# A hybrid decoder block on one core: the first stage scales x inside its transposing products, and moves part of its vector work

## The chip, the cores and the metric

The kernel runs on one core of a Trainium2 chip. The metric is the device time of one execution in microseconds (us). Engines: PE (TensorE, matrix products; PEld is its weight load), DVE (VectorE), ACT (ScalarE), POOL (GpSimd), SP (SyncE, which here only issues transfers). A name such as SPq or POOLq in a row is that engine's queue issuing a transfer.

## The reference

One decoder layer over 512 tokens of width 2048, all in float32. Only its first steps matter here:

```python
mod = jax.nn.silu(c) @ w_ada[l] + b_ada[l]              # c: (1, 2048), w_ada: 2048 x 12288
sh1, sc1, g1, sh2, sc2, g2 = jnp.split(mod, 6, axis=-1)
u = _modulate(_rmsnorm(h, norm_attn[l]), sh1, sc1)      # h * rsqrt(mean(h*h) + eps) * g, per token
z = u @ w_in                                            # 2048 x 5664
...
h = h + g1[:, None, :] * y                              # the plain h is needed again here
```

The rest (forgetting attention, sparse attention, the gated MLP, the last norm) is untouched by the change.

## The kernel before, in words

The program is one straight line per engine: every engine executes its own instructions in the order in which the Python code emits them, and waits at an instruction until its inputs are there. In the stage at hand the order is written out by hand, as a loop over steps.

**x.** x is 4 MB, as 4 blocks of 128 tokens (`t`), each loaded as two tiles of 128x1024 (L133) into the 8 buffers of the tag `adw`. PE transposes it in 128x128 pieces (L189, 64 transposes, 4 per PSUM bank); ACT and DVE copy the banks to `xT` (L194, L198), with channels on the partitions, and make the sums of squares beside it (L193, L196). When all four blocks are done, one short chain gives the token scale r = 1/sqrt(mean + eps) for all tokens (`rstd_of`, L163 to L169, a square root on ACT and one Newton step on DVE). PE broadcasts it over the partitions (`rows_of`, L175), and DVE multiplies it into each of the 16 channel tiles of xT (`norm_x`, L412), giving `xn`.

**w_ada.** The stage needs the first two of the six parts of mod (shift and scale): 32 MB of w_ada, in 64 slots of 512 KB. Slot n is loaded by SP (L513) into one of the 8 `adw` buffers as soon as its last user is done. 8 slots make a group `jj`, which gives 2x256 entries of mod, enough for two channel tiles. A slot holds two blocks of 128 rows. DVE multiplies each with its entry of silu(c) and adds it to `acc` (L538, L540). In 21 slots (`on_pe`) the second block goes to PE instead, as a 512-column product with a broadcast column (L550) whose row is copied (L554) and turned into columns (first half of L563). After a group, PE sums `acc` over the partitions as four single-column products (second half of L563), DVE adds the bias (`mod`, L571) and makes `a_vec` (L400), ACT makes u = xn * scale + shift twice (L418: a rounded high part and the full one), and DVE the low part (L423). The tables `LAGS` and `LAGS0` say how many steps after a group's last slot these follow.

**w_in.** Each tile of w_in is split into a high part (ACT, L244) and a low part (DVE, L249). A "unit" is three PE products of 128x512 (L278 to L280) into one bank. Units queue in `todo`; 1 to 3 are emitted per step, from step 39 on 3.

**Sine tables.** `tables` makes the cosine and sine tables for the rotary step in 19 pieces, 18 of them on DVE (L434 to L452); one piece is emitted per step, from step 14 on.

**The end of the stage.** SP writes the plain xT to DRAM (`xsp`, L602), since it is needed again much later, and the stage's memory is given up (`st.close()`). The rotary step of the keys (`roped`, L621 to L628) uses tiles in that memory, so it waits until those writes have landed; and PE's next products need the PSUM banks that it reads.

The code around the change, with the line numbers of the profile:

Of the kernel before, what the change touches and what calls it, by code (L numbers as in the profile page):

```python
# [29 lines left out]
LAGS0 = 1, 2, 3, 0  # L30
# [49 lines left out]
def hymba_block(ctx: ExitStack, tc: tile.TileContext, x, c, positions, w_ada, b_ada, norm_attn,  # L80
# [49 lines left out]
    for t in range(NT):  # L130
        for g in range(2):
            xt = early.tile([P, 2, T], F32, tag="adw", name=uid("xtok"), bufs=ADW)
            nc.sync.dma_start(xt, x[t * P:(t + 1) * P, g * 1024:(g + 1) * 1024].rearrange("p (a b) -> p a b", b=T))  # L133
            xtok[t, g] = xt
# [45 lines left out]
    ssq = con.tile([P, NT], F32, name="ssq")  # L180
    ssq4 = early.tile([P, NT, 4], F32, name="ssq4")
    xT = early.tile([P, ND, T], F32, name="xT")
    tags = BANKS_A + BANKS_B
    for t in range(NT):
        for g in range(4):
            src = xtok[t, g // 2][:, g % 2, :]
# [4 lines left out]
            junk = early.tile([P, T], F32, tag="mt", name=uid("junk"), bufs=2)  # L191
            if g % 2 == 0:
                nc.scalar.activation(junk, src, AF.Square, accum_out=ssq4[:, t, g:g + 1])  # L193
                nc.vector.tensor_copy(dst, b)  # L194
            else:
                nc.vector.scalar_tensor_tensor(junk, src, 1.0, src, op0=OP.mult, op1=OP.mult,  # L196
                                               accum_out=ssq4[:, t, g:g + 1])
                nc.scalar.copy(dst, b)  # L198
    nc.vector.tensor_reduce(ssq, ssq4, axis=AX.X, op=OP.add)
# [12 lines left out]
    rstd1 = rows_of(rstd_of(ssq, D, "rs1"), "mm", early.tile([P, T], F32, name="rstd1"))  # L212
# [196 lines left out]
    xn = [act.tile([P, T], F32, tag="al", name=f"xn{i}", bufs=ND) for i in range(ND)]  # L409

    def norm_x(i):
        nc.vector.tensor_tensor(xn[i], xT[:, i, :], rstd1, op=OP.mult)  # L412

    def modulate(i):
        h = act.tile([P, T], F32R, tag="ah", name=uid("uh"), bufs=ND)
        t = early.tile([P, T], F32, tag="mt", name=uid("mt"), bufs=2)
        for dst in (h, t):
            nc.scalar.activation(dst, xn[i], AF.Identity, scale=a_vec[:, 0, i:i + 1], bias=mod[:, i:i + 1])  # L418
        return h, t
# [8 lines left out]
    def tables():  # L428
        nonlocal cosT, sinT
        cosT = mid.tile([P, T], F32, tag="cos", name="cosT")  # L430
        sinT = mid.tile([P, T], F32, tag="sin", name="sinT")
        ang = posi.bitcast(F32)
        nc.scalar.copy(ang, posi)
        nc.vector.tensor_scalar(ang, ang, cs[:, K_FRQ:K_FRQ + 1], None, op0=OP.mult)  # L434
        yield
        for dst, turn in ((sinT, 0.0), (cosT, 0.25)):
            kk = mid.tile([P, T], F32, tag="wx", name=uid("kk"))
# [59 lines left out]
    def on_pe(n):  # L497
        j, r = divmod(n, 8)
        return r < 5 if j == 0 else j <= HJ and 2 <= r < 6

    tiles, accs, rows, sums, halves, fetched, todo = {}, {}, {}, {}, {}, {}, []
    extra_work = tables()
    AT, AT_END = {0: 0, 1: 1, 3: 2}, {0: 0, 1: 1, 5: 2}
    norms = {4: (0, 1), 5: (2,), 6: (3,), 8: (4, 5)}
    norms.update({9 + i: (6 + i,) for i in range(10)})
    step = 0
    while step < SLOTS + 8 or todo:
        j, r = divmod(step, 8)
        if j < NJ:
            tiles[step] = early.tile([P, 2, T], F32, tag="adw", name=uid("ad"), bufs=ADW)  # L510
            for i, sec in ((0, 1), (1, 0)):
                c0 = sec * D + j * 256
                nc.sync.dma_start(tiles[step][:, :, i * 256:(i + 1) * 256],  # L513
                                  w_ada[:, c0:c0 + 256].rearrange("(q p) n -> p q n", p=P)[:, 2 * r:2 * r + 2, :])
# [15 lines left out]
        if 0 <= n < SLOTS:  # L530
            jj, q0 = n // 8, 2 * (n % 8)
            if q0 == 0:
                accs[jj] = early.tile([P, T], F32, tag="acc", name=uid("acc"), bufs=2)
            acc = accs[jj]
            for q in range(1 if on_pe(n) else 2):
                sc1 = sl[:, q0 + q:q0 + q + 1]
                if q0 + q == 0:
                    nc.vector.tensor_scalar(acc, tiles[n][:, q, :], sc1, None, op0=OP.mult)  # L538
                else:
                    nc.vector.scalar_tensor_tensor(acc, tiles[n][:, q, :], sc1, acc, op0=OP.mult, op1=OP.add)  # L540
        if step in norms:
            for i in norms[step]:
                norm_x(i)
        n = step - 2
        if 0 <= n < SLOTS and on_pe(n):
            jj, q = n // 8, 2 * (n % 8) + 1
            first = n == 0 or not on_pe(n - 1)
            if first:
                rows[jj] = bank("mm")
            nc.tensor.matmul(rows[jj], sl[:, q:q + 1].to_broadcast([P, P]), tiles[n][:, 1, :],  # L550
                             start=first, stop=not on_pe(n + 1))
            if not on_pe(n + 1):
                row = early.tile([1, T], F32, tag="row", name=uid("row"), bufs=2)
                nc.scalar.copy(row, rows[jj][0:1, :])  # L554
                rows[jj] = row
        n = due(step, 0)
        if n is not None:
            jj = n // 8
            sums[jj] = bank("mm")
            srcs = ([(rows.pop(jj), one_col[0:1, :])] if jj in rows else []) + [(accs.pop(jj), one_col)]  # L560
            for av, one in srcs:
                for i in range(4):
                    nc.tensor.matmul(sums[jj][:, i:i + 1], av[:, i * P:(i + 1) * P], one,  # L563
                                     start=i == 0 and one is srcs[0][1], stop=one is one_col,
                                     skip_group_check=True)
# [28 lines left out]
        if step >= 14:  # L594
            next(extra_work, None)
# [5 lines left out]
    for i in range(ND):  # L601
        nc.sync.dma_start(xsp[i], xT[:, i, :])  # L602
# [836 lines left out]
```

## Time and profile before

| | |
|---|---|
| median of 3 runs | 2440.64 us (2437.82 to 2442.27) |
| the profiled execution | 2438.08 us, its span 2436.3 us, mean granted clock of PE 0.977 |
| busy over the span | PE 2349.1, DVE 1583.2, ACT 1026.5, POOL 341.2 us |
| the stage at hand | from 0 to about 180 us of the span |

All times of the trace count from the start of the span. PE is busy nearly everywhere, but a busy PE need not be a fast one, since the ends of products are modelled and its clock has two levels: a granted clock of 1.0 is 2.4 GHz, 0.5 is 1.2 GHz. So the stage is read engine by engine, by what each waits for.

### The profile page before, as it was taken

The page shows a single profiled execution, that of the slowest core. Times are in us where ns is not written, and L with a number is a line of the kernel's source. Part 1 is how long each engine was busy: PE and PEld are TensorE (multiplying, and loading weights), DVE is VectorE, ACT ScalarE, POOL GpSimd, SP SyncE. Part 2 cuts the span into 40 slices and gives each one's busy share as a digit, 9 for nine tenths or more (in the row PEclk, how much of TensorE's full clock was granted, in tenths as well). Part 3 has the DMA queues.
Part 4 walks back from the last instruction along what each step waited for, and adds up shares of the span by engine and source line. Part 5 has one row for each costly group of instructions (what it writes and reads, how often), then busy time and mean ns, then how long its engine had stood idle before and what let it go on. Part 6 is the DMA issues. An engine that isn't in the chain of part 4 may idle for free.

```text
span 2436.3 us, 38417 instructions
## 1 busy us (share of the span) xinstructions
PE 2349.1 (96%) x14677; PEld 2100.5 (86%) x14677; DVE 1583.2 (65%) x2719; ACT 1026.5 (42%) x1544; POOL 341.2 (14%) x370
## 2 busy tenths in 40 slices
PE   6998999999999999889999999999999999999998
PEld 4777887888887777789999999999999888888887
DVE  7867887787655566596777677777676633333333
ACT  3335444334323323365555555555555422222233
POOL 0002002000102021251222221212121100000010
PEclk8999999999999999899999999999999999999998
DMA  9974643453563287469898889988988644333322
GB/s 331 322 232 143 178 142 101 122 180 119 164 181 122 82 274 255 159 145 231 214 230 220 221 217 229 224 219 219 216 200 196 187 156 141 121 117 122 105 94 99
DMA packets 322713, 440.31 MB, mean 181 GB/s; under 512 B 26224, under 2 KB 217552, under 8 KB 322528
## 3 DMA queue, kind: packets, MB, share of 16 engines
q1 hardware_dynamic: 289104, 348.21, 44.3%
q0 software_dynamic: 31120, 85.45, 18.9%
q10 hardware_dynamic: 2304, 4.20, 0.5%
q8 instruction: 115, 1.88, 0.3%
q14 instruction: 70, 0.57, 0.1%
HBM read 340.18 MB, written 28.38 MB: 151 GB/s over the span
## 4 chain that ended last, share of the span: by engine, by line
PE 55%; DVE 1%; DMA 0%; issue 0%; ACT 0%; SPq 0%; DVEq 0%; ACTq 0%
PE py L1173 12%; PE py L1176 11%; PE py L1175 11%; PE psmm L278 3%; PE psmm L280 3%; PE psmm L279 3%; PE pss L278 2%; PE pss L279 2%; PE pss L280 2%; PE pso L278 1%; PE pso L279 1%; PE pso L280 1%; DMA wr<-in_w_down_dram 0%; PE pso L1070 0%; DVE ul L1153 0%
## 5 line engine op out<-in xcount | busy, mean ns | idle before, releaser
L249 DVE TENSOR_TENSOR wl<-wr,wh 128x1024 fp32r<-128x1024 f32 (+2 forms) x211 | 238.8, 1132 | 371.1 <-ACT wh L244 369.5
L244 ACT CAST wh<-wr 128x1024 fp32r<-128x1024 f32 (+2 forms) x211 | 199.7, 948 | 528.9 <-PE psmm L279 204.0
L1176 PE MATMUL py<-uh,ls 128*128 128x256 f32 x1408 | 398.4, 283 | 2.8 <-DVE ls L1119 2.8
L1173 PE MATMUL py<-uh,hs 128*128 128x256 f32 x1408 | 399.3, 284 | 0.9 <-DVE ev L1190 0.5
L1175 PE MATMUL py<-ul,hs 128*128 128x256 f32 x1408 | 398.4, 283 | 1.8 <-DVE ul L1153 1.8
L1113 ACT CAST hs<-sum 128x1024 fp32r<-128x1024 f32 x176 | 184.6, 1049 | 377.0 <-PE py L1175 256.6
L1119 DVE TENSOR_TENSOR ls<-sum,hs 128x1024 fp32r<-128x1024 f32 x176 | 215.3, 1223 | 196.3 <-ACT hs L1113 196.3
L1175 PE MATMUL py<-ul,hx 128*128 128x256 f32 x1056 | 298.7, 283 | 4.1 <-DVE ul L1153 4.1
L1173 PE MATMUL py<-uh,hx 128*128 128x256 f32 x1056 | 299.3, 283 | 1.7 <-ACT uh L1152 1.4
L1176 PE MATMUL py<-uh,lx 128*128 128x256 f32 x1056 | 298.3, 282 | 0.0
L1176 PEld LDWEIGHTS py<-uh,ls 128*128 128x128 f32 x1408 | 268.0, 190 | 3.6 <-DVE ls L1119 3.6
L1173 PEld LDWEIGHTS py<-uh,hs 128*128 128x128 f32 x1408 | 268.1, 190 | 2.7 <-DVE ev L1190 1.3
L1175 PEld LDWEIGHTS py<-ul,hs 128*128 128x128 f32 x1408 | 268.0, 190 | 2.7 <-DVE ul L1153 2.7
L1109 POOL DMA_DIRECT2D lx<-raw x176 | 156.1, 887 | 579.2 <-ACT lx L1108 431.8
L1175 PEld LDWEIGHTS py<-ul,hx 128*128 128x128 f32 x1056 | 200.8, 190 | 4.9 <-DVE ul L1153 4.8
L1173 PEld LDWEIGHTS py<-uh,hx 128*128 128x128 f32 x1056 | 200.6, 190 | 2.2 <-ACT uh L1152 1.7
L1176 PEld LDWEIGHTS py<-uh,lx 128*128 128x128 f32 x1056 | 200.6, 190 | 0.0
L386 DVE SCALAR_TENSOR_TENSOR acc<-ad,sl,acc 128x512 f32<-128x512 f32 x180 | 143.2, 796 | 41.7 <-DMA ad<-in_w_ada_dram 40.1
L1108 ACT ACTIVATE lx<-raw 128x768 fp32r<-128x768 f32 x176 | 148.0, 841 | 1.8 <-DMA raw<-in_w_gate_dram 1.8
L1104 ACT CAST hx<-raw 128x768 fp32r<-128x768 f32 x176 | 144.4, 820 | 9.0 <-DMA raw<-in_w_gate_dram 9.0
L278 PE MATMUL psmm<-fh,wh 128*128 128x512 f32 x352 | 137.0, 389 | 0.0
L280 PE MATMUL psmm<-fh,wl 128*128 128x512 f32 x352 | 136.9, 389 | 0.0
(442 smaller groups left out, 5290.4 us busy)
## 6 DMA issues: line engine op xcount, KB each, us to landing
lx<-raw POOLq DMA_DIRECT2D x176, 384.0 KB, 5.2
ad<-in_w_ada_dram SPq DMA_DIRECT2D x128, 512.0 KB, 3.9
raw<-in_w_up_dram SPq DMA_DIRECT2D x176, 256.0 KB, 4.1
raw<-in_w_gate_dram SPq DMA_DIRECT2D x176, 256.0 KB, 4.4
wr<-in_w_down_dram SPq DMA_DIRECT2D x88, 512.0 KB, 3.7
ad<-in_w_ada_dram SPq DMA_DIRECT2D x128, 256.0 KB, 6.0
wr<-in_w_in_dram SPq DMA_DIRECT2D x104, 256.0 KB, 3.4
wr<-in_w_in_dram SPq DMA_DIRECT2D x24, 512.0 KB, 4.9
```

What stands on the lines that cost most here:

```text
L244: nc.scalar.copy(wh[:, :, sc], v)
L249: nc.vector.tensor_tensor(held[1][:, :, sc], v, split_ap(held[0])[:, :, sc], op=OP.subtract)
L278: nc.tensor.matmul(dst, wh[:, k, w], ah, start=first, stop=False)
L279: nc.tensor.matmul(dst, wh[:, k, w], al, start=False, stop=False)
L280: nc.tensor.matmul(dst, wl[:, k, w], ah, start=False, stop=last)
L1108: nc.scalar.activation(lx[s], raw[s][:, 1:4, :], AF.Copy, scale=-1.0)
L1109: nc.gpsimd.dma_start(split_ap(lx[s]), raw[s][:, 1:4, :], accum_op=OP.add)
L1113: nc.scalar.copy(hs[s], sums[s])
L1119: nc.vector.tensor_tensor(ls[s], sums[s], split_ap(hs[s]), op=OP.subtract)
L1173: nc.tensor.matmul(o, wh[:, wi, js], vh[:, vi, :], start=k == 0 and j == 0, stop=False, skip_group_check=True)
L1175: nc.tensor.matmul(o, wh[:, wi, js], vl[:, vi, :], start=False, stop=False, skip_group_check=True)
L1176: nc.tensor.matmul(o, wl[:, wi, js], vh[:, vi, :], start=False, stop=k == KG - 1, skip_group_check=True)
```

## The change

- x is loaded as 16 tiles of 128x512 into buffers of the tag `al` (free until the first low parts of u), so the 8 `adw` buffers are free for w_ada from the start.
- Each block of 128 tokens gets its own token scale (`token_scale`: nine DVE operations and a square root on ACT), which is put on the diagonal of a 128x128 tile. `turn` multiplies each piece of x with that diagonal as an ordinary fp32 product: this transposes and scales at once. Three of four banks are copied by ACT and one by DVE (before: half each). `norm_x`, `xn` and the broadcast at the start are gone. `std` keeps 1/r.
- PE's share of w_ada falls from 21 to 14 blocks (slots 0 to 5, 10 to 13, 18 to 21), and is made like the sum of `acc`: four products of one column each, straight into the group's bank. The 512-column products, their rows and the copies are gone.
- `LAGS0` is 1, 1, 2 in place of 1, 2, 3.
- The tables start at step 60 in place of 14, two pieces per step.
- At step 56 PE broadcasts `std`; from step 66 on DVE multiplies two tiles of xT per step with it, which gives the plain x again, and POOL (not SP) writes each to `xsp`.

```diff
-LAGS0 = 1, 2, 3, 0
+LAGS0 = 1, 1, 2, 0
+TAB = 60
...
+    def token_scale(t):
+        v, r, s = (early.tile([P, 1], F32, name=uid("rs1")) for _ in range(3))
+        nc.vector.tensor_reduce(v, ssq4[:, t, :], axis=AX.X, op=OP.add)
+        nc.vector.tensor_scalar(v, v, 1.0 / D, EPS, op0=OP.mult, op1=OP.add)
+        nc.scalar.activation(s, v, AF.Sqrt)
...
+        nc.vector.scalar_tensor_tensor(r, s, 1.5, r, op0=OP.add, op1=OP.mult)
+        diag = early.tile([P, P], F32, tag="diag", name=uid("diag"), bufs=2)
+        nc.vector.tensor_scalar(diag, ident, r, None, op0=OP.mult)
+        nc.vector.scalar_tensor_tensor(std[:, t:t + 1], v, -2.0, r, op0=OP.mult, op1=OP.mult)
+        return diag
+
+    def turn(t, diag):
+        for g in range(4):
             b = bank(tags[(t * 4 + g) % 8], (P, 4, P))
             for i in range(4):
-                nc.tensor.transpose(b[:, i, :], src[:, i * P:(i + 1) * P], ident)
+                nc.tensor.matmul(b[:, i, :], xtok[t, g][:, i * P:(i + 1) * P], diag, start=True, stop=True)
...
+    squares(0)
+    for t in range(NT - 1):
+        diag = token_scale(t)
+        squares(t + 1)
+        turn(t, diag)
...
-        return r < 5 if j == 0 else j <= HJ and 2 <= r < 6
+        return r < 6 if j == 0 else j < 3 and 2 <= r < 6
...
+    def plain_x(i):
+        nc.vector.tensor_tensor(xT[:, i, :], xT[:, i, :], stdr[0], op=OP.mult)
+        nc.gpsimd.dma_start(xsp[i], xT[:, i, :])
+
+    for n in range(3):
+        load_ada(n)
+    diag = token_scale(NT - 1)
+    accumulate(0)
+    turn(NT - 1, diag)
...
-            nc.tensor.matmul(rows[jj], sl[:, q:q + 1].to_broadcast([P, P]), tiles[n][:, 1, :],
-                             start=first, stop=not on_pe(n + 1))
...
+            columns(n // 8, tiles[n][:, 1, :], sl[:, q:q + 1], False)
...
-        if step >= 14:
-            next(extra_work, None)
+        if step >= TAB:
+            for _ in range(2):
+                next(extra_work, None)
+        if step == SLOTS - 8:
+            std_row()
+        if step >= SLOTS + 2:
+            for _ in range(2):
+                if plain:
+                    plain_x(plain.pop(0))
...
-    for i in range(ND):
-        nc.sync.dma_start(xsp[i], xT[:, i, :])
```

Where the order of an engine's instructions matters, it stands here as the programs have it; numbers behind a name count tiles.

DVE, between the last token scale and the first group's sums. Before:

```order
L168 TENSOR_TENSOR rs1s<-rs1s,rs_259 128x4
L169 SCALAR_TENSOR_TENSOR rs1r<-rs1s,rs1r 128x4
L538 TENSOR_SCALAR acc_308<-ad_302,sl 128x512
L540 SCALAR_TENSOR_TENSOR acc_308<-ad_305,sl,acc_308 128x512
L540 SCALAR_TENSOR_TENSOR acc_308<-ad_310,sl,acc_308 128x512
L540 SCALAR_TENSOR_TENSOR acc_308<-ad_316,sl,acc_308 128x512
L412 TENSOR_TENSOR xn_278<-xT,rstd_269 128x512
L412 TENSOR_TENSOR xn_279<-xT,rstd_269 128x512
```

and now:

```order
L203 SCALAR_TENSOR_TENSOR rs_71_312<-rs_72_313,rs_71_312 128x1
L205 TENSOR_SCALAR diag_322<-cs,rs_71_312 128x128
L206 SCALAR_TENSOR_TENSOR std<-rs_70_311,rs_71_312 128x1
L540 TENSOR_SCALAR acc_325<-ad_302,sl 128x512
L216 COPY xT<-pso_345 128x4x128
L542 SCALAR_TENSOR_TENSOR acc_325<-ad_305,sl,acc_325 128x512
L542 SCALAR_TENSOR_TENSOR acc_325<-ad_308,sl,acc_325 128x512
L542 SCALAR_TENSOR_TENSOR acc_325<-ad_357,sl,acc_325 128x512
```

One slot's product now stands between the diagonal and a copy from PSUM of the last products made with it, and the rest of the group stands behind that copy. In the three blocks ahead, the two squares of the next block (L191) stand in its place.

DVE again, at the end of the stage, from the last slot's sum on. Before:

```order
L249 TENSOR_TENSOR wl_1324<-wr_1241,wh_1323 128x768
L571 TENSOR_TENSOR mod<-psmm_1342,vec 128x2 x2
L400 SCALAR_TENSOR_TENSOR a_vec<-mod,vec 128x2
L423 TENSOR_TENSOR ul_1385<-mt_1360,uh_1359 128x512
L423 TENSOR_TENSOR ul_1387<-mt_1364,uh_1363 128x512
L249 TENSOR_TENSOR wl_1339<-wr_1246,wh_1338 128x1024
```

and now:

```order
L273 TENSOR_TENSOR wl_1347<-wr_1252,wh_1346 128x768
L459 TENSOR_SCALAR kk_1362<-kk_1362 128x512
L461 TENSOR_SCALAR kk_1362<-kk_1362 128x512
L601 TENSOR_TENSOR mod<-psmm_1368,vec 128x2 x2
L424 SCALAR_TENSOR_TENSOR a_vec<-mod,vec 128x2
L465 SCALAR_TENSOR_TENSOR cosT<-kk_1362,posi 128x512
L465 SCALAR_TENSOR_TENSOR cosT<-kk_1362,cosT 128x512
L558 TENSOR_TENSOR xT<-xT,stdr 128x512 x2
L465 SCALAR_TENSOR_TENSOR cosT<-kk_1362,cosT 128x512 x2
L558 TENSOR_TENSOR xT<-xT,stdr 128x512 x2
L442 TENSOR_TENSOR ul_1425<-mt_1388,uh_1387 128x512
```

Pieces of the tables (L457 to L471) stand on both sides of the last `mod`, and the 16 products that restore x (L558) stand behind it, two by two between the rest of the tables, the low parts and the next splits of w_in.

PE, at the first group of w_ada. Before:

```order
L175 MATMUL psmm_270<-cs,rs1r 128x128 x4
L550 MATMUL psmm_314<-ad_302,sl 128x512
L550 MATMUL psmm_314<-ad_305,sl 128x512
L550 MATMUL psmm_314<-ad_310,sl 128x512
L550 MATMUL psmm_314<-ad_316,sl 128x512
L550 MATMUL psmm_314<-ad_321,sl 128x512
L563 MATMUL psmm_363<-cs,row_341 128x1 x4
L563 MATMUL psmm_363<-cs,acc_308 128x1 x4
```

and now:

```order
L213 MATMUL pso_345<-diag_322,xtok_113 128x128 x4
L549 MATMUL psmm_352<-sl,ad_302 128x1 x4
L549 MATMUL psmm_352<-sl,ad_305 128x1 x4
L549 MATMUL psmm_352<-sl,ad_308 128x1 x4
L549 MATMUL psmm_352<-sl,ad_357 128x1 x4
L549 MATMUL psmm_352<-sl,ad_365 128x1 x4
L549 MATMUL psmm_352<-sl,ad_373 128x1 x4
L549 MATMUL psmm_352<-cs,acc_325 128x1 x4
```

The single-column products of six slots stand behind the last block's products with the diagonal; before, five 512-column products stood behind one short broadcast.

## Rows read from the trace of the kernel before

**Rows 1.** Busy time of each engine in three stretches; columns as headed.

```profile
core 0: us, PE busy (x) PEld busy (x) DVE busy (x) ACT busy (x) POOL busy (x), PEclk, DMA share, GB/s
23.79:154.15 130.36, 120.42 (x491) 90.58 (x492) 122.94 (x198) 44.87 (x59) 0.00 (x0) 0.91 0.98 316
38.30:65.00 26.70, 21.37 (x78) 14.56 (x79) 26.52 (x46) 8.83 (x12) 0.00 (x0) 0.88 1.08 347
65.00:157.60 92.60, 92.60 (x396) 72.40 (x395) 83.06 (x129) 33.32 (x43) 0.00 (x0) 0.94 0.92 295
```

**Rows 2.** Timeline, last slot and last group: start, duration, engine, line, [idle before <- releaser].

```profile
152.62 1.53 DVE L540 SCALAR_TENSOR_TENSOR acc<-ad,sl,acc 128x512 f32<-128x512 f32 x2
...
157.67 0.95 PE L563 MATMUL psmm<-cs,acc 128*128 128x1 f32 x8
...
158.65 0.23 DVE L571 TENSOR_TENSOR mod<-psmm,vec 128x2 f32<-128x2 f32 x2 [3.63 <-PE psmm L563]
```

**Rows 3.** Line L602 by itself, and the timeline where the stage is left.

```profile
L602 SPq DMA_DIRECT2D xsp<-xT x16: 423/649/934, 164.3 to 174.8; - x16
...
179.00 0.59 ACT L621 ACTIVATE sw<-psmm 64x512 f32<-64x512 f32 x1 [2.84 <-DMA xsp<-xT]
...
180.97 0.63 PE L278 MATMUL psmm<-uh,wh 128*128 128x512 f32 x1 [2.30 <-DVE r L623]
```

**Rows 4.** Timeline of the start, from the first tile of x to the first unit.

```profile
6.79 0.63 ACT L193 ACTIVATE junk<-xtok 128x512 f32<-128x512 f32 x1 [2.93 <-DMA xtok<-in_x_dram]
...
9.30 0.63 ACT L193 ACTIVATE junk<-xtok 128x512 f32<-128x512 f32 x1
...
18.28 1.47 PE L189 MATMUL pss<-cs,xtok 128*128 128x128 f32 x12
...
21.50 1.28 ACT L164 ACT_TABLE_LOAD   x1
...
21.88 0.17 DVE L199 TENSOR_REDUCE ssq<-ssq 128x4 f32<-128x16 f32 x1
...
23.03 0.17 DVE L165 TENSOR_SCALAR rs<-rs 128x4 f32<-128x4 f32 x1 [0.57 <-ACT rs1s L164]
...
23.79 0.49 DVE L538 TENSOR_SCALAR acc<-ad,sl 128x512 f32<-128x512 f32 x1
...
23.92 1.87 PE L175 MATMUL psmm<-cs,rs1r 128*128 128x128 f32 x8 [3.21 <-DVE rs1r L169]
...
38.34 0.80 PE L278 MATMUL pss<-uh,wh 128*128 128x512 f32 x1 [2.37 <-ACT uh L418]
```

**Rows 5.** Busy time of each engine around L175; columns as in rows 1.

```profile
23.80:27.20 3.40, 3.28 (x10) 2.33 (x11) 3.29 (x7) 0.58 (x1) 0.00 (x0) 0.56 1.10 348
```

**Rows 6.** Timeline of PE: a 512-column product of w_ada, and single columns.

```profile
34.23 1.73 PE L563 MATMUL psmm<-cs,acc 128*128 128x1 f32 x8 [1.48 <-DVE acc L540]
...
98.25 0.40 PE L280 MATMUL pss<-uh,wl 128*128 128x512 f32 x1
98.49 1.02 PE L550 MATMUL psmm<-ad,sl 128*128 128x512 f32 x2
...
99.58 0.39 PE L279 MATMUL pss<-ul,wh 128*128 128x512 f32 x1
...
103.55 1.05 PE L563 MATMUL psmm<-cs,row 1*128 1x1 f32 x8
104.53 1.05 PE L563 MATMUL psmm<-cs,acc 128*128 128x1 f32 x8
```

**Rows 7.** Groups by line, DVE, 23.8 to 151.6: count | busy us, mean ns | idle.

```profile
L540 DVE SCALAR_TENSOR_TENSOR acc<-ad,sl,acc 128x512 f32<-128x512 f32 x97 | 72.7, 750 | 2.2
...
L412 DVE TENSOR_TENSOR xn<-xT,rstd 128x512 f32<-128x512 f32 x16 | 10.8, 684 | 0.0
...
L446 DVE SCALAR_TENSOR_TENSOR sinT<-kk,sinT 128x512 f32<-128x512 f32 x3 | 2.1, 687 | 0.0
```

**Rows 8.** Line L1109, POOL's transfers beside a busy DVE: ns minimum/median/maximum, and landing.

```profile
L1109 POOL DMA_DIRECT2D lx<-raw x176: 847/849/1175, 960.5 to 1908.2; - x176
...
DMA to landing us min/median/max: 3.9/5.2/8.1
```

More of the change, by code (lines that the diff above doesn't have):

```diff
@@ L130, in hymba_block @@
     for t in range(NT):
[L131 to L134, printed above, removed]
+        for g in range(4):
+            xtok[t, g] = act.tile([P, T], F32, tag="al", name=uid("xtok"), bufs=ND)
+            nc.sync.dma_start(xtok[t, g], x[t * P:(t + 1) * P, g * T:(g + 1) * T])
     rows1 = early.tile([P, P], F32, name="rows1")
@@ L498, in on_pe, with load_ada, accumulate, columns @@
         j, r = divmod(n, 8)
-        return r < 5 if j == 0 else j <= HJ and 2 <= r < 6
-    tiles, accs, rows, sums, halves, fetched, todo = {}, {}, {}, {}, {}, {}, []
+        return r < 6 if j == 0 else j < 3 and 2 <= r < 6
+    tiles, accs, sums, halves, fetched, todo = {}, {}, {}, {}, {}, []
     extra_work = tables()
     AT, AT_END = {0: 0, 1: 1, 3: 2}, {0: 0, 1: 1, 5: 2}
-    norms = {4: (0, 1), 5: (2,), 6: (3,), 8: (4, 5)}
-    norms.update({9 + i: (6 + i,) for i in range(10)})
+    def load_ada(n):
+        j, r = divmod(n, 8)
+        tiles[n] = early.tile([P, 2, T], F32, tag="adw", name=uid("ad"), bufs=ADW)
+        for i, sec in ((0, 1), (1, 0)):
+            c0 = sec * D + j * 256
+            nc.sync.dma_start(tiles[n][:, :, i * 256:(i + 1) * 256],
+                              w_ada[:, c0:c0 + 256].rearrange("(q p) n -> p q n", p=P)[:, 2 * r:2 * r + 2, :])
+    def accumulate(n):
+        jj, q0 = n // 8, 2 * (n % 8)
+        if q0 == 0:
+            accs[jj] = early.tile([P, T], F32, tag="acc", name=uid("acc"), bufs=2)
+        acc = accs[jj]
+        for q in range(1 if on_pe(n) else 2):
+            sc1 = sl[:, q0 + q:q0 + q + 1]
+            if q0 + q == 0:
+                nc.vector.tensor_scalar(acc, tiles[n][:, q, :], sc1, None, op0=OP.mult)
+            else:
+                nc.vector.scalar_tensor_tensor(acc, tiles[n][:, q, :], sc1, acc, op0=OP.mult, op1=OP.add)
+    def columns(jj, src, one, last):
+        first = jj not in sums
+        if first:
+            sums[jj] = bank("mm")
+        for i in range(4):
+            nc.tensor.matmul(sums[jj][:, i:i + 1], src[:, i * P:(i + 1) * P], one,
+                             start=first and i == 0, stop=last, skip_group_check=True)
+    stdr = []
+    def std_row():
+        stdr.append(rows_of(std, "mm", early.tile([P, T], F32, name="stdr")))
+    def plain_x(i):
[6 more added lines that the diff above has]
+    turn(NT - 1, diag)
+    plain = list(range(ND))
     step = 0
@@ L508, in hymba_block @@
         j, r = divmod(step, 8)
[L509 to L514, printed above, removed]
+        if j < NJ and step not in tiles:
+            load_ada(step)
         if r == (3 if j else 7) and j < NJ:
@@ L529, in hymba_block @@
         n = step - 1
[L530 to L543, printed above, removed]
+        if 1 <= n < SLOTS:
+            accumulate(n)
         n = step - 2
         if 0 <= n < SLOTS and on_pe(n):
[L546 to L549, printed above, removed]
-            nc.tensor.matmul(rows[jj], sl[:, q:q + 1].to_broadcast([P, P]), tiles[n][:, 1, :],
-                             start=first, stop=not on_pe(n + 1))
[L552 to L555, printed above, removed]
+            q = 2 * (n % 8) + 1
+            columns(n // 8, tiles[n][:, 1, :], sl[:, q:q + 1], False)
         n = due(step, 0)
         if n is not None:
[L558 to L565, printed above, removed]
+            columns(n // 8, accs.pop(n // 8), one_col, True)
         n = due(step, 1)
@@ L600, in hymba_block @@
             z_first[0] = lambda w=w: w
-    for i in range(ND):
-        nc.sync.dma_start(xsp[i], xT[:, i, :])
+    for i in plain:
+        plain_x(i)
+    for _ in extra_work:
+        pass
     st.close()
```

31 lines of the change are left out of this document (16 added, 15 removed).

## The prediction

> **What bounds the kernel now.** I read four views: the busy times by stretch, the timeline of the stage's two ends, the groups of DVE's instructions, and the timeline of the start.
>
> Backwards from the end: PE stops at 178.7 and goes on only at 180.97, when DVE has read a bank of the rotary step; that step on ACT had waited until 179.0 for the last write of `xsp` [rows 3]. The writes stand behind the last group's `mod`, at 158.65. So the stage is left 179.0 - 158.65 = 20.35 us after the last `mod`, whatever was fast before. Call the last `mod` M.
>
> What sets M? DVE is busy 122.94 of the 130.36 us from its first slot of w_ada (23.79) to the end of its last one, 152.62 + 1.53 = 154.15 [rows 1, 2]. The transfers run beside it at a share of 0.98, 316 GB/s, and PE is busy without a gap from 65 on [rows 1]. The last sum over the partitions starts on PE at 157.67, and DVE waits 3.63 us for it [rows 2]. So three chains end close together: DVE's work, PE some 3 us behind it, and the transfers a little ahead. A gain on one is capped by the next. The reader should see here that DVE was the chain to relieve, and that relief only counts if DVE starts as early as before.
>
> **The change, part by part.**
>
> *DVE's work between its first and last slot of w_ada.* The 16 `norm_x` go: 10.8 us of busy time [rows 7], some 10.3 without the overlap of neighbours. Ten of the 18 table operations move behind the last slot: four of the eight large ones at 0.687 [rows 7] and six small ones; with overlap I put it at 4.5 (bounds 4 and 5). Seven slots' second blocks come back from PE: 7 x 0.75 = 5.2 [rows 7]. The first slot's product (0.5) is done earlier. 122.9 - 10.3 - 4.5 + 5.2 - 0.5 = 112.8 us of work: 10.1 less.
>
> *When this work can start.* Before: at 23.79, right behind the token scale. Now the rest of the first group stands behind the copy of the last block's products, and so do, block after block, the next scale, products and copy. DVE cannot step over a copy that waits for PE, so the four blocks add up:
> - The first block is there at about 8.5 (its first half before 6.79, its second by 9.30, [rows 4]). A square 0.8, the table load 1.3 and the root 0.2 on ACT give 10.8. From the root to the finished scale DVE took 0.9 (23.03 to 23.92), the diagonal adds 0.3 (an estimate from the small operations): the products start at 12.0.
> - One product: four 128x128 fp32 products took 1.87 us at a granted clock of 0.56, so near 1.2 GHz: 0.43 each with the tail off [rows 4, 5]. At 2.4 GHz no row shows one. The nearest is the 512-column one: from 98.25 to 99.58 are two ordinary products of 0.23 and it, so 0.87, a quarter of which is 0.22 [rows 6]. Sixteen take 6.9 us at the low clock, 3.5 at the high one. PE has idled before the first block, so I take 5.2 there (the clock rises halfway), and 4.2 for the others, between 3.5 and 6.9 and nearer the first, since PE pauses only some 2.6 us between blocks.
> - So copy of block 0 done at 12.0 + 5.2 + 0.7 = 17.9. Each further block: scale 1.9 (reduce, small operations and root as in [rows 4], no table load, diagonal), products 4.2, copy 0.7: 6.8. Two small copies add 0.5. 17.9 + 3 x 6.8 + 0.5 = 38.8, say 39.
>
> The start moves from 23.8 to 39: 15.2 us later. Bounds: 34.5 (first products at 11, 3.5 throughout after a first 4.5), and 48.6 (6.9 everywhere).
>
> The Trainium skill says, in "TensorE: Matmul & The Clock Gate", Terms, that the transpose mode is "4× faster for FP32"; this change leaves that mode. By that rule a product would cost four of the transposes' 1.47 / 12 = 0.12 us [rows 4], 0.49, and a block 7.8, which by itself would put the start near 51. The row of L550 (0.22) speaks against it.
>
> *What DVE waits for after that.* Nine sums end near 46. PE then has single columns to finish: eight records took 1.73 us after a pause and 0.9 to 0.98 in the midst of work [rows 6]; six slots from 38.3 on take between 5.5 and 10.4, I take 8, and the sum over `acc` 1.7: first `mod` at 48, two us after DVE is free (36.9 before), first unit at 49.5 in place of 38.34 [rows 4]. With 1.5 us for other waits (before: 7.4 in all, most of them for PE) the last slot ends at 39 + 112.8 + 3.5 = 155.3, before 154.15.
>
> *PE.* Behind its first unit it loses 16 products of 0.87 and four rows of 0.98, 17.8, and gets eight slots of 0.92 and the broadcast of `std` (0.9): 9.5 less. It starts 11.2 later, but had idled 26.70 - 21.37 = 5.3 in the first stretch [rows 1]. 157.67 - 9.5 + 11.2 - 5.3 = 154.1: now just ahead of DVE, so its saving is not on the path.
>
> *Transfers.* x no longer occupies the w_ada buffers, so slots 0 to 7 and the first w_in tiles are loaded by about 29 (9.3 MB at 350 GB/s). Then slot 8 waits for slot 0's users, near 39: this head start is thrown away. 38 MB are left; at the 347 GB/s of [rows 1] they end near 148, 7 us ahead of DVE's end. SP has only these loads behind it. Cost 0; the cover is DVE's 155.
>
> *M.* Behind the last slot DVE has a split and four small table operations, 2.4 us: M = 157.7, against 158.65: 0.95 earlier.
>
> *From M to leaving the stage.* DVE: `mod` 0.4, six table operations 3.1, two low parts 1.3, two splits 2.3, sixteen plain tiles 10.3 (as `norm_x`): 17.4. POOL issues each write while DVE makes the next; behind them on POOL stand only the rotary products, which wait for the writes anyway. Landing 4.1 to 5.2 after an issue (179.0 less 174.8 on SP's queue, [rows 3]; 5.2 on POOL's, [rows 8]): 21.5 to 22.6, in place of 20.35. I take 1.6 us longer. ACT's copies (12 instead of 8) and the later sine step lie beside it: 0.
>
> **Sum.** -0.95 + 1.6 = +0.7 us. The profiled execution took 2438.08, 2.6 under the median of 2440.64, so 2438.8 to 2441.3: I forecast **2440 us**, no change that can be told. That is 0.2%, 4.9 us, either way of the median.
>
> **Rivals.**
>
> *A, the start goes well.* High clock from the middle of the first block on, x early: start at 34.5 (-4.5), columns at 0.92 (-1.2), writes landing in 4.1 (-0.6): -5.6, about **2435 us**. For it: PE's pauses between blocks are short, and in 38 to 65 the clock held 0.88 in spite of 5.3 us idle. Against: PE was at 1.2 GHz after each longer pause of the start [rows 5].
>
> *B, slower: DVE is held by slow products.* If sixteen products take 6.9 us in every block, because PE falls to 1.2 GHz in each pause, the start is at 48.6 and the sum +10.3: **2451 us**. It decides from a start at 43 on, 5.6 us per block. For: rows 5. Against: a block's products are work that raised the clock in the trace. The skill's factor of four would give nearly the same (start 51, 2453), and is a second way here.
>
> *C, POOL's writes stall.* POOL writes `xsp` while DVE is busy. If each issue cost several times its 0.85 us [rows 8], the sixteen would end long after DVE: at 3 us each the stage is left some 33 us later, **2473 us**. Against: [rows 8] is such a queue beside a busy DVE, and its slowest issue is 1.18. "SBUF — State Buffer", section on a bandwidth-pool intuition, in the Trainium skill, says that such a transfer can take 3.1 us beside a VectorE copy that locks a shared port; the rows do not bear it out.
>
> **Chances.** The forecast 0.49, A 0.28, B 0.20, C 0.03. The forecast's own spread is some 4 us either way (start, table overlap, landing), so a little of it falls on either side of 0.2%, and B has lesser forms within it. Faster 0.32, same 0.44, slower 0.24. The range 2430 to 2452 holds the forecast's case, most of A (with 3 us for the overlap I took off `norm_x` and the tables) and B's price.
>
> **What would show it.** In the profile of the changed kernel: L216's last copy for x ends near 38 and L542 starts right behind it; sixteen L213 products take 4 to 5 us; the first unit (L302) starts near 49; the last L542 ends near 155; the last `mod` (L601) at 157 to 158 with little wait; the first L660 on ACT some 22 us later, waiting for `xsp`. I am wrong if the products of a block take 3.5 or less or 6 and more, if DVE's work after the start is not near 113 us, or if something other than the writes holds the end of the stage.

## The result, and the profile after

The changed kernel takes 2461.25 us (median of 6, 2454.23 to 2462.39), the kernel before, beside it, 2439.51 (2435.65 to 2442.27): a ratio of 1.0084, 95% interval 1.0073 to 1.0094. It is slower by some 20 us. The forecast was 2440, the range 2430 to 2452.

The profiled execution took 2457.68 us, its span 2455.9, 19.6 longer than before's. Both programs have the same instructions behind the first stage, so the start of one instruction in both traces shows where the time goes:

| stretch | before | after | longer by |
|---|---|---|---|
| start to the first copy of the rotary step (the first stage is left) | 179.00 | 187.58 | 8.6 |
| from there to the last modulated tile of the gated MLP (`ur`, some 30 us behind the MLP's first product) | 879.7 | 886.1 | 6.4 |
| from there to the MLP's last gathered weights | 848.4 | 854.0 | 5.6 |
| the rest | | | -1.0 |

So there are three questions, and two of them lie in code that the change does not touch.

The start, in the timeline (start, duration, engine, line, [idle before <- releaser]):

```profile
11.55 6.18 PE L213 MATMUL psmm<-diag,xtok 128*128 128x128 f32 x32 [7.83 <-DVE diag L205]
...
34.58 2.92 PE L213 MATMUL pss<-diag,xtok 128*128 128x128 f32 x24 [2.49 <-issue]
...
38.22 8.27 PE L549 MATMUL psmm<-sl,ad 128*128 128x1 f32 x48
38.43 0.69 DVE L216 COPY xT<-pso 128x512 f32<-128x512 f32 x1 [3.48 <-PE pso L213]
39.03 7.04 DVE L542 SCALAR_TENSOR_TENSOR acc<-ad,sl,acc 128x512 f32<-128x512 f32 x9
...
48.23 0.23 DVE L601 TENSOR_TENSOR mod<-psmm,vec 128x2 f32<-128x2 f32 x2 [2.16 <-PE psmm L549]
49.55 0.79 PE L302 MATMUL pss<-uh,wh 128*128 128x512 f32 x1 [1.36 <-ACT uh L437]
```

This is the start as forecast (39, 48, 49.5). The reader should see the releaser of the copy: DVE stands 3.48 us behind PE. The end, which answers to [rows 2, 3]:

```profile
162.56 1.53 DVE L542 SCALAR_TENSOR_TENSOR acc<-ad,sl,acc 128x512 f32<-128x512 f32 x2
...
166.34 0.22 DVE L601 TENSOR_TENSOR mod<-psmm,vec 128x2 f32<-128x2 f32 x2
...
187.58 0.59 ACT L660 ACTIVATE sw<-psmm 64x512 f32<-64x512 f32 x1 [4.59 <-DMA xsp<-xT]
```

The last slot ends at 164.09 (forecast 155.3), the last `mod`, called M as before, stands at 166.34 (forecast 157.7), and the stage is left 21.2 us behind it. Between the start and the end, the busy times by stretch; columns as in [rows 1]:

```profile
24.00:40.00 16.00, 11.03 (x97) 10.60 (x95) 7.50 (x30) 7.10 (x15) 0.00 (x0) 1.00 0.59 188
40.00:58.00 18.00, 15.42 (x58) 13.48 (x58) 15.18 (x24) 5.33 (x7) 0.00 (x0) 0.53 1.03 330
58.00:80.00 22.00, 22.00 (x137) 19.24 (x137) 18.67 (x28) 4.61 (x6) 0.00 (x0) 1.00 0.95 299
80.00:140.00 60.00, 51.39 (x223) 41.45 (x222) 57.95 (x90) 21.81 (x28) 0.00 (x0) 0.94 1.09 353
39.03:164.09 125.06, 112.78 (x530) 93.84 (x529) 115.47 (x178) 39.59 (x52) 0.00 (x0) 0.90 0.96 308
```

and the first of them in the trace of before:

```profile
24.00:40.00 16.00, 10.61 (x35) 6.62 (x35) 15.68 (x27) 5.47 (x8) 0.00 (x0) 0.72 1.10 351
```

Four things to see. From 24 to 40 the transfers run at 188 GB/s in place of 351. PE's clock is 0.53 from 40 to 58, behind the first single columns. From 80 to 140 the transfers are at 353 GB/s, the most of these stretches, while PE idles 8.6 us. DVE is busy for 115.5 us and idle for 9.6, where 112.8 and 3.5 were forecast. DVE's waits behind the first `mod`:

```profile
66.31 0.23 DVE L601 TENSOR_TENSOR mod<-psmm,vec 128x2 f32<-128x2 f32 x2 [0.60 <-PE psmm L549]
...
69.67 0.69 DVE L442 TENSOR_TENSOR ul<-mt,uh 128x512 fp32r<-128x512 f32 x1 [0.72 <-ACT mt L437]
...
71.94 0.75 DVE L542 SCALAR_TENSOR_TENSOR acc<-ad,sl,acc 128x512 f32<-128x512 f32 x1 [0.77 <-DMA ad<-in_w_ada_dram]
73.39 1.54 DVE L542 SCALAR_TENSOR_TENSOR acc<-ad,sl,acc 128x512 f32<-128x512 f32 x2 [0.70 <-DMA ad<-in_w_ada_dram]
...
101.44 4.69 DVE L542 SCALAR_TENSOR_TENSOR acc<-ad,sl,acc 128x512 f32<-128x512 f32 x6 [0.49 <-DMA ad<-in_w_ada_dram]
...
147.13 0.22 DVE L601 TENSOR_TENSOR mod<-psmm,vec 128x2 f32<-128x2 f32 x2 [0.83 <-PE psmm L549]
```

Only 2.0 us of them are for transfers. With 2.16 for the first `mod`, 1.4 for PE at two later ones and 1.0 for ACT (two pauses of 0.13 at `ul` counted in) that makes 6.5 of the 9.6. The other 3.1 us are 86 gaps of less than 0.1 us, nearly all between an accumulation and the next one that needs it; in the trace of before there are 63 of them, 2.3 us.

The transfers' gap stands in SP's timeline (transfers in one row follow each other without a wait):

```profile
20.16 6.33 SPq L529 DMA_DIRECT2D ad<-in_w_ada_dram  x9
26.88 1.87 SPq L249 DMA_DIRECT2D wr<-in_w_in_dram  x3
39.21 4.78 SPq L529 DMA_DIRECT2D ad<-in_w_ada_dram  x8
```

From 28.75 to 39.21 SP issues nothing: slot 8 needs slot 0's buffer, and PE reads that from 38.22 on.

For the MLP, one row of its products in the trace of before (engine, operation, count: ns minimum/median/maximum, first and last start):

```profile
L1173 PE MATMUL py<-uh,hs x1408: 274/283/415, 1029.0 to 1925.7; 128*128 128x256 f32 x176
```

and of after:

```profile
L1212 PE MATMUL py<-uh,hs x1408: 278/283/415, 1044.1 to 1946.4; 128*128 128x256 f32 x176
```

The same products take 896.7 us before and 902.3 after. The mean distance of neighbouring starts, from all starts of MLP products between 1080 and 1890 us less than 140 ns apart, is 119.15 ns before and 119.98 after. The only difference that reaches them is where their tiles lie. The change drops four small tiles (`ssq`, and three of the old token scale, 32 bytes of every partition each) from the pool of constants, and every tile allocated behind them moves down by 128 bytes.

### The profile page after: what moved, and what is told of

The parts are those of the page before. It is cut to its first block, busy times and chain, and to the rows that moved or that the text cites. A ratio compares the mean times of both kernels' runs of the same rounds, so it can differ in the third digit from the quotient of the medians.

```text
span 2455.9 us, 38634 instructions
## 1 busy us (share of the span) xinstructions
PE 2345.8 (96%) x14771; PEld 2108.4 (86%) x14771; DVE 1593.3 (65%) x2751; ACT 1027.9 (42%) x1546; POOL 350.7 (14%) x386
## 4 chain that ended last, share of the span: by engine, by line
PE 54%; DVE 1%; DMA 1%; issue 0%; ACT 0%; SPq 0%; DVEq 0%; ACTq 0%
PE py L1212 11%; PE py L1214 11%; PE py L1215 11%; PE psmm L302 3%; PE psmm L304 3%; PE psmm L303 3%; PE pss L302 2%; PE pss L303 2%; PE pss L304 2%; PE pso L304 1%; PE pso L302 1%; PE pso L303 1%; DMA wr<-in_w_down_dram 0%; DVE ul L1192 0%; DMA hr<-hd 0%
```

## The experiments

Fifteen runs, two of them second profiles of the two kernels as they are. "M late" is the start of the last `mod` less before's 158.65; "MLP" is the span of the row above (L1173 in before), both from the run's one profile; "ratio" is to the kernel before on the same chip.

| run | kernel | M late | MLP | ratio, interval |
|---|---|---|---|---|
| | the change | 7.7 | 902.3 | 1.0084 (1.0073 to 1.0094) |
| e1 | change, addresses of before | 8.6 | 896.7 | 1.0054 (1.0037 to 1.0071) |
| e2 | before, -128 bytes | -3.4 | 902.4 | 1.0034 (1.0019 to 1.0049) |
| e3 | change, 512-column products | 8.7 | 902.4 | 1.0083 (1.0065 to 1.0101) |
| e4 | change with plain transposes | 2.6 | 896.7 | 1.0028 (1.0015 to 1.0041) |
| e5 | e1, six more slots ahead | 4.4 | 896.1 | 1.0041 (1.0026 to 1.0055) |
| e6 | e4 with 512-column products | 0.2 | 896.7 | 1.0026 (1.0010 to 1.0042) |
| e7 | before, -64 bytes | -2.8 | 893.3 | 0.9987 (0.9975 to 0.9999) |
| e8 | before again (one profile) | 0.7 | 896.7 | |
| e9 | e3, six more slots ahead | 11.5 | 902.4 | 1.0091 (1.0071 to 1.0111) |
| e10 | change, -64 bytes | 8.1 | 893.3 | 1.0034 (1.0023 to 1.0046) |
| e11 | before, -32 bytes | -1.5 | 902.2 | 1.0028 (1.0016 to 1.0039) |
| e12 | before, -96 bytes | -3.1 | 893.1 | 0.9966 (0.9953 to 0.9978) |
| e13 | e5, last copy on ACT | 5.4 | 896.7 | 1.0020 (1.0003 to 1.0037) |
| e14 | the change again (one profile) | 8.0 | 902.3 | |
| e15 | e13, -96 bytes | 2.2 | 892.2 | 0.9996 (0.9983 to 1.0009) |

**Addresses.** e1 puts the dropped bytes back into the changed kernel; e2 takes them out of the kernel before.

```diff
+    pads = [con.tile([P, NT], F32, name="ssq")]
...
+    pads += [con.tile([P, NT], F32, name="rs1" + s) for s in ("", "r", "s")]
+    for p in pads:
+        nc.gpsimd.memset(p, 0.0)
```

```diff
+        pl = early if name == "rs1" else con
...
-    ssq = con.tile([P, NT], F32, name="ssq")
+    ssq = early.tile([P, NT], F32, name="ssq")
```

> The changed kernel with four small tiles that nobody reads put back at the places of the four that the change dropped from the pool of constants, so that every tile of the later stages lies again at the address that it had in the kernel before (all addresses had moved by 128 bytes per partition). Theory 'addresses': the 11 us that are lost behind the first stage are lost because of that shift, so the time falls to 2448 to 2454 us, the matrix products of the gated MLP start again every 120.2 ns in the mean with a spread, and the first stage alone stays 8 us late. Theory 'not the addresses' (what is lost later follows from the order or the timing that the first stage leaves): the time stays at 2457 to 2462 us and the products at 120.76 ns.

> The kernel before, with the four small tiles of the token scale moved from the pool of constants to the stage's own pool; nothing else. All later tiles move by 128 bytes per partition, as the change moves them. Theory 'addresses': 6 to 11 us slower than before, 2446 to 2451 us, with the loss behind the first stage only. Theory 'not the addresses': 2440 us, within 3.

Measured: e1 2454.66 us, some 7 less than the change, with the MLP at 896.7; e2 2446.52, 8 more than before by the ratio, with the MLP at 902.4. The theory of the addresses holds both ways for the MLP, and 5.6 us of the 20 are theirs; but not for all of the 11 us that are lost behind the stage, as e1's forecast had it. e7, e10, e11 and e12 move or drop other numbers of the same tiles (e7: `ssq` and one more to the stage's pool; e10: two kept in the changed kernel):

> The kernel before with two of the four small tiles of the token scale moved out of the pool of constants, so that every later tile moves by 64 bytes per partition in place of 128. Theory 'any shift from this layout costs': 2445 to 2448 us and the MLP's products every 120.4 ns or more, as with 128 bytes. Rival 'only some places cost': 2440 us within 2.

> The changed kernel with 64 bytes per partition put back in the pool of constants, so that the later tiles lie where they lay in the run of before with 64 bytes less. Theory 'addresses set the pitch of the MLP's products': 118.5 to 118.6 ns, the MLP 9 us shorter than in the changed kernel, the time 2450 to 2453 us. Rival 'the pitch hangs on more than the addresses': 119 ns or more, 2455 us or more. The first stage stays 7 to 9 us late by both.

> The kernel before with one of the four small tiles moved out of the pool of constants: later tiles 32 bytes lower. With this, tiles of the MLP begin at multiples of 64 bytes, which they did not at 0, -64 and -128. Theory 'alignment to 64 bytes decides': a pitch of 118.5 ns or less and 2430 to 2434 us. Rival 'the 64-byte grid plays no part': a pitch between 118.6 and 120 ns and 2433 to 2445 us.

> The kernel before with three of the four small tiles moved: later tiles 96 bytes lower, and the MLP's moving tiles begin at multiples of 512 bytes. Theory 'alignment decides': the shortest pitch of all, under 118.5 ns, and 2428 to 2433 us. Rival 'the grid plays no part': between 118.6 and 120 ns, 2433 to 2447 us.

e7 refutes that any shift costs: -64 gains. e10 has e7's MLP, 893.3, in another kernel, so the place alone sets it. e11 refutes my rule of alignment to 64 bytes, and e12, whose 118.54 ns falls between its two forecasts, does not save it: -32 and -128 are slow, -64 and -96 fast. The trace of e12:

```profile
L1174 PE MATMUL py<-uh,hs x1408: 277/281/415, 1028.1 to 1921.2; 128*128 128x256 f32 x176
```

Mean distances are 119.15, 119.96, 118.61, 118.54 and 119.98 ns at 0, -32, -64, -96 and -128 bytes. Which of the tiles matters, and why, was not tried. e12 is 0.34% faster than before, the fastest kernel of the study.

**The head start of the transfers.** e5 loads slots 8 to 13 into tiles that are idle until the first high parts of u (and has before's addresses):

```diff
+        if 8 <= n < 8 + HEAD:
+            tiles[n] = [act.tile([P, T], F32, tag="ah", name=uid("ad"), bufs=ND) for _ in range(2)]
```

> The changed kernel with six more slots of w_ada (8 to 13, 3 MB) loaded into tiles that lie idle until the first high parts of u, so that SP need not wait for the users of slot 0 near 39 us; and with every later tile at its address of before (the four small tiles back, and the tables ahead of the kept half in their pool). Theory 'the transfers lose their head start': between 24 and 40 us the transfers run at 300 GB/s or more in place of 188, and the last slot's sum ends 5 to 8 us earlier than 164.1, at 156 to 159; with the first run's 2454.7 that gives 2446 to 2450 us. Rival 'DVE and PE' (PE at its low clock from 51 to 68 us, and DVE's own late start): the transfers are early, and the last slot's sum still ends at 162 us or later. On the addresses: the attention stages lose 0 to 1 us against before where the run with the four tiles alone lost 2, if the tables' place matters; else 2 again.

```profile
24.00:40.00 16.00, 11.79 (x91) 11.55 (x91) 7.58 (x30) 6.20 (x13) 0.00 (x0) 0.89 0.98 309
...
38.20:160.80 122.60, 110.56 (x530) 91.75 (x529) 115.32 (x178) 39.63 (x52) 0.00 (x0) 0.92 0.94 302
```

The transfers run at 309 GB/s from 24 to 40, and M comes 4.2 us earlier than in e1. Not all of that is the head start: DVE went on at 38.20 in place of e1's 39.21. DVE's waits for slots, 2.6 us in e1 and 2.0 in the change, are gone; so the lost head start costs some 3 us. The last slot ends at 160.8, between the two forecasts: I had put this share too high. (The low clock that the rival speaks of lies at 40 to 58 in the change, as the rows above show, not at 51 to 68.) 4.4 us remain. On the tables' place the run says nothing: the stretch behind the stage is 884.4 us, as long as e1's 884.6.

**Single columns.** e3 makes PE's 14 blocks as 512-column products again; e4 undoes the scaling in the transposing products; e6 is both.

```diff
-            columns(n // 8, tiles[n][:, 1, :], sl[:, q:q + 1], False)
...
+            nc.tensor.matmul(rows[jj], sl[:, q:q + 1].to_broadcast([P, P]), tiles[n][:, 1, :],
...
+                nc.scalar.copy(row, rows[jj][0:1, :])
```

```diff
-        turn(t, diag)
...
+                nc.tensor.transpose(b[:, i, :], src[:, i * P:(i + 1) * P], ident)
...
+        if step in norms:
+            for i in norms[step]:
+                norm_x(i)
```

> The changed kernel with PE's 14 blocks of w_ada made as in the kernel before: 512-column products into a row, the row copied and turned into columns. Theory 'single columns hold the buffers' (in the first groups they run at the low clock and keep the w_ada buffers from SP, so the transfers fall behind): the last slot's sum ends 3 to 6 us earlier than the 164.1 of the changed kernel, and the time falls by as much, to 2455 to 2458 us. Theory 'the start' (the transfers fall behind because DVE frees the first buffers only from 39 us on): the last slot's sum ends within 2 us of 164.1, or later.

> The changed kernel without the scaling in the transposing products: plain transposes, one token scale for all four blocks, its product into the 16 channel tiles in the steps of the kernel before, and xT written out by SP as before. x in its own buffers, the 14 blocks as single columns, the late tables and the shorter lags stay. The four small tiles are back too, so the later addresses are those of before. Theory 'the start': DVE starts on w_ada near 24 us, the last slot's sum ends at 151 to 156 us, the stage is left at 176 to 180 us, and with the later stages as before the time is 2436 to 2442 us. Theory 'single columns hold the buffers': the last slot's sum ends at 158 us or later, the time 2444 us or more.

> The fourth run's kernel (plain transposes, one token scale, x in its own buffers, late tables) with PE's 14 blocks as 512-column products and a row again, and the tables at their place of before. Theory 'single columns leave PE at its low clock': in the fourth run the clock was 0.58 from 60 to 80 us, and the transfers lost 3.6 us there; with rows it is 0.9 or more, the last slot's sum ends 3 to 5 us earlier than in the fourth run, and the time is 2440 to 2444 us. Rival 'the products are not the cause of the clock': the clock falls there again, and the time stays at 2447 to 2450 us.

In e4 and e6 the two forms stand side by side. e4, then e6, from 59 to 77 us:

```profile
59.00:77.00 18.00, 17.10 (x60) 14.53 (x60) 11.45 (x16) 4.29 (x6) 0.00 (x0) 0.53 0.90 284
```

```profile
59.00:77.00 18.00, 17.07 (x64) 12.22 (x64) 12.74 (x21) 5.80 (x9) 0.00 (x0) 0.81 1.08 346
```

With single columns PE stands near 1.2 GHz and the transfers fall to 284 GB/s; with 512-column products it is 0.81 and 346, and M comes 2.5 us earlier. I take that as the price of the single columns there, with a reservation: e6 also has the tables' tiles at their place of before, and each is one profile. That the columns act through the clock is how I read the two rows. By e4's own numbers its second theory holds (last slot at 159.0, time 2448.55). Yet the start counts more: without the scaling in the products M is 6.0 earlier than in e1, with the columns still there.

In the changed kernel the exchange buys nothing: e3's M is no earlier than the change's, its last slot ends at 165.05, as its second theory had it, and its transfers have the same gap (191 GB/s from 24 to 40). e9 adds the head start to it:

> The changed kernel with both: six more slots of w_ada loaded ahead, and PE's 14 blocks as 512-column products (at the addresses of the changed kernel, the tables' place of before). Theory 'two losses, one behind the other' (the lost head start hides the low clock of the single columns): the last mod, 4.4 us later than before with the head start alone, comes 1 to 2.5 later; the low clock behind the first group lasts 7 us or less in place of 14; the time, with the 6 us of the addresses still in it, is 2446 to 2450 us. Rival 'DVE's late start holds it': the last mod stays 4 us or more late, 2450 to 2453 us.

The time, 2461.14 us, misses both forecasts, and M is 11.5 late, the worst of all. The trace of e9 shows two new waits (DVE first, then ACT):

```profile
41.99 0.69 DVE L217 COPY xT<-pso 128x512 f32<-128x512 f32 x1 [6.41 <-PE pso L214]
...
47.14 0.57 ACT L608 COPY row<-psmm 1x512 f32<-1x512 f32 x1 [5.84 <-PE psmm L604]
47.62 1.04 ACT L269 CAST wh<-wr 128x1024 fp32r<-128x1024 f32 x1
```

The copy of the row waits 5.84 us at the head of ACT's queue, and behind it stands the first split of w_in, which starts at 47.62; in the changed kernel it starts at 38.01. And the last block's products came late in this execution (the clock was low from 34 to 42). So rows have a price of their own here, and this run does not isolate the low clock's share.

**DVE's late start.** e13 moves the copy at 38.43 from DVE to ACT, for the last block alone.

```diff
-            if g == 3:
+            if g == 3 and t < NT - 1:
```

> The fifth run's kernel (six more slots loaded ahead, addresses of before), with the last block's fourth bank copied by ACT in place of DVE, so that DVE goes from the first slot to the next without waiting for PE's products. Theory 'DVE's late start': DVE goes on near 34 us in place of 38.2, and the last mod comes 2.5 to 4 us earlier than in the fifth run, 0.5 to 2 us behind before's 158.65. Rival 'the transfers and the low clock set the end': DVE is early by 4 us, loses it in later waits, and the last mod moves by less than 1 us.

```profile
34.70 7.05 DVE L555 SCALAR_TENSOR_TENSOR acc<-ad,sl,acc 128x512 f32<-128x512 f32 x9
...
37.95 8.25 PE L562 MATMUL psmm<-sl,ad 128*128 128x1 f32 x48
...
47.94 0.23 DVE L614 TENSOR_TENSOR mod<-psmm,vec 128x2 f32<-128x2 f32 x2 [6.19 <-PE psmm L562]
```

In this profile the rival holds. DVE goes on at 34.70 in place of 38.2, and then waits 6.19 us for PE's columns: the first `mod` stays at 47.9 (47.2 in e5). In this first group the chain is PE: its last products of x, 48 single columns, the sum. But PE was slower here than in e5: its columns took 8.25 us, with a granted clock of 0.77 from 38 to 42, and 5.73 in e5, with 1.00. So this pair does not show what freeing DVE is worth, and by the ratios e13 is, if anything, the faster (1.0020 against 1.0041, intervals that overlap). e15 is e13's program at other addresses:

> The thirteenth run's kernel with its later tiles 96 bytes lower, where before's were in the twelfth run, the fastest layout seen. Theory 'the losses add up': the MLP 3.6 us shorter than before's, the first stage as in the thirteenth run, 2438 to 2444 us. Rival 'a gain in one place is lost in the next': 2444 us or more.

```profile
34.63 7.05 DVE L554 SCALAR_TENSOR_TENSOR acc<-ad,sl,acc 128x512 f32<-128x512 f32 x9
...
37.88 5.74 PE L561 MATMUL psmm<-sl,ad 128*128 128x1 f32 x48
...
45.36 0.23 DVE L613 TENSOR_TENSOR mod<-psmm,vec 128x2 f32<-128x2 f32 x2 [3.68 <-PE psmm L561]
```

Here the columns run at 1.00 from 38 to 42, as in e5, and DVE is free, as in e13. The first `mod` comes 2.6 us earlier than in e13, and M 3.1: that is what the earlier and longer low clock cost there (from 52 to 58 the granted clock is 0.57 in e13 and 0.91 in e15). Against e5, with columns as quick, the first `mod` comes 1.8 earlier and M 2.2: that is what the free DVE gains once PE keeps pace. In the first group of the changed kernel DVE's nine sums end at 46.07 and PE's columns at 46.49; two chains end together, and relieving one of them shows little. These are single profiles, and whether the addresses or the execution set the moment at which the clock fell is not shown.

With the best layout, this form of the change takes 2436.43 us, no different from before, and 0.3% behind e12, which has nothing of the change.

**Between the stages.** e8 and e14 are second profiles of both kernels.

> The kernel before, unchanged: a second profile, to see how far the stages of one kernel vary between executions. If the last mod of the first stage lies within 1 us of 158.65 and the span from there to the first product of the MLP within 1 us of the first profile, differences of 3 us between kernels in these places count; if not, they don't.

> The changed kernel, unchanged: a second profile. If the time from the end of the first stage to the MLP's first modulated tile is again 6 us longer than in the first profile of before, the change costs something there; if it comes out within 3 us of before's, the difference lies within what executions of one kernel differ by.

The first stage repeats: M at 0.7 and 8.0. The stretch behind it does not. It takes 879.7 and 878.9 us in the two profiles of before, 881.8 to 885.9 in e2, e7, e11 and e12, which have before's instructions; 886.1 and 880.1 in the two of the change, 878.6 to 888.4 in its variants. By the bound set for e8, 3 us would have counted; by e14 they don't. Of the 6.4 us, I can assign none to the change. That the median is slower by 20 and the stage and the MLP explain 14 says that something remains. e2, before's instructions at the change's addresses, keeps a rest of the same size: 8 us by the ratio, where its MLP loses 5.7 and its first stage gains 3.4. But e1, at before's addresses, is slower by 13, where its first stage explains 9.6. So what remains is open.

## Why the prediction was wrong

**The start: right, its parts less so.** Products at 11.55 (12.0), the last copy ends at 39.1 (39), the first `mod` at 48.23 (48), the first unit at 49.55 (49.5). The four blocks took 6.2, 5.3, 3.8 and 3.8 us (5.2 and three times 4.2): PE was at the high clock from 24 to 40. The first block lies beyond the 6 that was named as a sign of being wrong, and none took the 4 to 5 us; slower first blocks and quicker last ones nearly made up for each other, which is luck in part. The two prices were right: in the trace of the change products started 0.43 us apart until 16.4, and 0.22 apart in the last two blocks. With its share of the tail one product there takes 0.24 us, twice a transpose's 0.12 and not four times. The Trainium skill's factor of four ("TensorE: Matmul & The Clock Gate", Terms), weighed in the prediction, is not what the traces show for these 128x128 pieces.

**"112.8 us of work": 2.7 us short.** This is the first step that failed, a term of the sum that was mis-sized. The sum took the 16 `norm_x` at 10.3 us, their duration less some overlap. Their price was lower, as the trace of before shows:

```profile
45.15 0.74 DVE L540 SCALAR_TENSOR_TENSOR acc<-ad,sl,acc 128x512 f32<-128x512 f32 x1
45.81 0.68 DVE L412 TENSOR_TENSOR xn<-xT,rstd 128x512 f32<-128x512 f32 x1
46.41 0.74 DVE L540 SCALAR_TENSOR_TENSOR acc<-ad,sl,acc 128x512 f32<-128x512 f32 x1
```

Two accumulations with `xn` between them start 1.26 us apart. Without it they start 0.79 apart ((7.04 - 0.75) / 8, from the nine above): each must wait for the one before. So `norm_x` cost 1.26 - 0.79 = 0.47 each, 7.5 in all, and removing them gave 2.8 less than I booked: 2.1 of it in busy time (1.26 - 0.75 each), the rest as new gaps between accumulations. The tables between accumulations were booked in the same way.

**"With 1.5 us for other waits" and "Transfers: cost 0; the cover is DVE's 155": wrong, 6.1 us.** This is the step that failed most inside the stage: 3.5 us of idle DVE were forecast with the first `mod`, 9.6 came. Half of the difference, 3.1 us, are the short gaps between dependent accumulations, which the sum put at nothing. They stood in the trace of before too (2.3 of the 7.4), and "most of them for PE" misread it: 1.0 us is a wait for PE, 2.0 one for ACT, which had itself waited for PE, and the rest is for ACT alone. ACT's wait:

```profile
99.55 0.57 ACT L554 COPY row<-psmm 1x512 f32<-1x512 f32 x1 [6.00 <-PE psmm L550]
100.03 0.83 ACT L244 CAST wh<-wr 128x768 fp32r<-128x768 f32 x1
```

The other half are waits: 2.0 us for transfers, 1.4 for PE at later groups, 1.0 for ACT, where 1.5 was allowed. The prediction saw that the head start is thrown away, and then let 7 us of slack in the transfers pay for it. The gap was (351 - 188) GB/s over 16 us, 2.6 MB or 7.4 us of transfers. The slack at the end was there: SP had issued the last slot by 148.3, and DVE came to it at 162.56. But a cover over the whole stage does not feed each slot in time: DVE stood for single slots at 71.9, 73.4 and 101.4, and being busy 97% from 80 on it does not win such waits back. e5 shows that the waits go with the head start, some 3 us in M. The prediction priced the columns (8 us, measured 8.27) but not what the low clock does behind them: at the higher clock they take 5.7, and between e13 and e15 that and the units behind are worth 3.1 us of M.

164.09 - 155.3 = 8.8 is 2.7 of work and 6.1 of waits, and M is 8.6 later than forecast.

**From M to leaving the stage: right.** 21.2 us, a little under the 21.5 to 22.6. POOL's 16 issues took 0.54 us each: rival C is out. The 3.1 us that the Trainium skill states ("SBUF — State Buffer", on the bandwidth-pool intuition) are for a transfer beside a VectorE copy; DVE made no copy while POOL issued these, so this run does not test that figure.

**PE: right where it was claimed.** The last `mod` no longer waits for PE (3.63 in [rows 2]).

**What the sum left out: the later stages.** The prediction added up one stage and took the rest as equal, since their instructions are. 5.6 us came from there through the addresses (e1, e2), and some 6 more are not explained. That is a missing term, not a mis-sized one: the removed `con` tiles were in plain sight in the change.

Rival B gave 2451 by slow products in every block. Only the first block came near its 6.9 us, and the start was as forecast; the time is higher for other reasons.

## What to carry to other kernels

Tiles dropped from a long-lived pool move everything behind them: compare the addresses of both programs before pricing a change, and try a few 32-byte shifts, since 96 bytes alone were worth 0.3% here. Slack of the transfers at the end of a stage does not pay for a gap at its start, where the engine that uses them is near full; look at which buffer the next load waits for. An instruction that stands between links of a dependent chain costs less than its duration, so removing it gains less, and the links then stand apart by gaps that a sum of durations leaves out. And where two chains end together, an experiment that relieves one of them can show nothing; look whether the other ran as fast in both traces.

## What the runs showed that was not expected

- The spacing of identical fp32r products in the MLP hangs on where their tiles lie, in steps of 32 bytes: 118.54 to 119.98 ns, and the same in different kernels: 896.7 us for the MLP in six of seven profiles with before's layout, 896.1 in the other.
- The first stage of the unchanged kernel was also faster in the profiles of other layouts (M 1.5 to 3.4 earlier in e2, e7, e11 and e12): in both profiles of before the clock falls three times between 71 and 112 us, in e2 not, and M is 3.4 earlier. That the layout is the cause is not shown. From 80 to 120, before and then e2:

```profile
80.00:120.00 40.00, 40.00 (x166) 30.35 (x165) 34.06 (x53) 15.54 (x21) 0.00 (x0) 0.91 1.02 327
```

```profile
80.00:120.00 40.00, 39.81 (x180) 30.48 (x178) 36.07 (x56) 15.96 (x22) 0.00 (x0) 1.00 1.03 330
```

- In DVE's queue an instruction starts 0.08 us before the end of an independent one ahead of it, and 0.035 us after the end of one that it depends on (medians in the trace of before, from 23.8 to 154.2 us).
